# Reordering the start of a feed-forward block: an accumulating transfer behind a norm, an activation table at the beginning, squares and gated units behind later weights

## The chip, the cores and the metric

The kernel runs on one core of a Trainium2 chip. The metric is the device time of one execution in microseconds (us), as the median of several runs; lower is better. The core has five engines that work side by side and wait for each other through semaphores: TensorE (PE in the profile) multiplies matrices, VectorE (DVE) and ScalarE (ACT) work elementwise, GpSimd (POOL) does small things and issues some DMA transfers, and SyncE (SP) issues most transfers. Each engine executes its own instructions in one order.

## The reference

A trunk of two layers is applied with the same weights to a prompt of 512 tokens and a sample group of 256, each token a vector of 1024. Every layer is: half a SwiGLU feed-forward block, a mixer (attention and gating; not touched here), half a SwiGLU block again. At the end stands a norm. So there are four feed-forward blocks in all:

```python
def rmsnorm(x, g):
    return x * lax.rsqrt(jnp.mean(x * x, axis=-1, keepdims=True) + EPS) * g

def swiglu(h, wg, wu, wd):                      # wg, wu: 1024 x 2816, wd: 2816 x 1024
    return (jax.nn.silu(h @ wg) * (h @ wu)) @ wd

x = x + 0.5 * swiglu(rmsnorm(x, f1_n), f1_g, f1_u, f1_d)
x = x + mixer(rmsnorm(x, mix_n), ...)
x = x + 0.5 * swiglu(rmsnorm(x, f2_n), f2_g, f2_u, f2_d)
```

All of it is in float32.

## The kernel before

The 768 tokens stand side by side as columns, in two **halves** of 384 (`HALVES`, L25); the 1024 features are eight tiles of 128 rows. For float32 accuracy each operand is split in a high and a low part and each product is three matmuls: high by high, low by high, high by low (`mm3`, L230). The weight's parts are made in `wsplit` (L147): ScalarE casts the high part (`whi`, L163) and VectorE subtracts it (`wlo`, L164). So PE needs ScalarE and then VectorE for each piece of 128 x 512 weights, and the third matmul of a product is the first to need `wlo`. There are five buffers for each part.

A feed-forward block (`ffn`, L458) goes through the 2816 hidden features in 11 **pairs** of 256 (`pair`, L509). A pair's products with gate and up weights go over tokens in two halves and features in two halves, and a scheme of the Strassen kind makes seven products of the eight. Their activation operands are named in the trace `b11`, `b21`, `t2`, `t3`, `t1`, `b22` and `n4`, and are sums or differences of halves of x with the gain in them; their weights are sums and differences too (`sums`, L711). A **product** here is one of the seven, for gate and for up, 24 matmuls of 128x384: `p1` (`b11`), `p2` (`b21`), `p6` (`t2`), `p7` (`t3`), `p5` (`t1`), `p3` (`b22`) and `p4` (`n4`). The norm's scale of a token is applied after the products, in the gated units: `hidden(i, half, g, u)` (L579) multiplies gate and up by the scale, takes Silu of the gate and multiplies them. It is three VectorE instructions (L585, L587, L588) and one of ScalarE (L586), and it waits until the norm of that half is known (L581).

The block's start: pairs 0, 1 and 2 (`EARLY = 3`) run `p1` and `p2` before everything else, in the sequence of `ORDER` (L42), so that PE has work while the other operands are made (`feed`, `rest`). Then pair 0 runs `t2`, `t3`, `t1`, `b22`, `n4`, then pair 1 the same five, then pair 2.

- *The norm.* ScalarE squares the eight tiles of a half and VectorE adds seven of them up (`norm_add`, L263); PE sums over rows (`norm_tok`, L282), GpSimd takes the power -0.5 (`power`, L311, the instruction of L314), PE spreads the result over partitions (`norm_spread`, L298, the transposes of L198), and ScalarE copies it to `acc` (L455). In the first block the delays `DELAYS` (L34) say after how much PE work, counted at 0.16 us a matmul, the sums and then the spreading are put into PE's order. The first block's second half of squares is made in `squares` (L435).
- *Weight sums by DMA.* `wsum` (L138) loads one weight with SyncE and adds another to it with an accumulating transfer that GpSimd issues (L144). `load_all` (L525) issues all transfers of a pair: ten plain ones (for pair 0, whose first weights are there already, six) and four accumulating ones.
- *The second stage.* `operands` (L475) makes from a pair's gated units the operands of the down projection, in 11 steps. They are taken one at a time: the next pair calls `next(steps)` after certain of its products.
- *What is put behind a product.* `self.after[p, b]` holds functions that are called right after the up weights of pair p's product b have been split; `later` (L595) files pair 0's gated units of the second half this way.

**What sets the order.** The order of PE is that of the program. The instructions of the other engines are ordered by a list scheduler at build time: of those whose inputs and buffers are ready in its model, the one that the program issued first goes first. `issue_after(i)` adds the condition that what stands in the block comes behind instruction i on the same engine; it is an order and not a wait between engines. `high_priority()` puts an instruction ahead of others. The tiles named `e` (30 of them) and `s` (8) are rings whose buffers become free when the last reader is done.

The lines that set the sequence of the start:

```python
        stages = [pair(p) for p in range(NPAIR)]
        for p in ORDER:
            next(stages[p])
        units = [lambda: next(stages[1]), lambda: next(stages[2])]
        if behind:
            self.after[0, "t1"] = [self.squares] + units
        else:
            self.after[0, "t3"] = units
        self.after[0, "n4"] = [lambda: next(stages[1])]
```

`behind` is true in the first feed-forward block alone.

## Time and profile before

| what | value |
|---|---|
| median of 3 runs | 2585.97 us (2585.16 to 2588.82) |
| the profiled execution | 2585.71 us, of them 2583.9 in the profile's span |
| mean granted clock of PE | 0.997 |
| PE busy | 2557.8 us, 99% of the span |
| DVE busy | 2099.9 us, 81% |
| ACT busy | 1370.6 us, 53% |
| POOL busy | 323.3 us, 13% |

The profile is one execution, taken by the hardware profiler. A row of a timeline has the start in us from the beginning of the span, the duration in us, the engine, the line of the kernel, the operation, output <- inputs, how many such instructions are merged in the row, and in brackets how long the engine was idle before it and what ended that. A row of waits has the sum, the count and the longest. Buffer numbers are left out of the names: `whi` and `wlo` are the two parts of a weight, `t20h` is the high part of the first tile of `t2`. Matmuls are pipelined, so the next one starts before the row's duration is over.

### The profile page before, as it was taken

How to read it: one execution, taken by the hardware profiler on the slowest of the kernel's cores; microseconds unless marked ns; L12 is line 12 of the kernel's file. 1: busy time of each engine (PE TensorE's matmuls, PEld its weight loads, DVE VectorE, ACT ScalarE, POOL GpSimd, SP SyncE). 2: the span in 40 equal slices, each digit the busy share in tenths (PEclk: the TensorE clock that was granted, in tenths of full speed). 3: DMA queues.
4: the chain of work that ended last, by engine and by line, in shares of the span. 5: the costliest groups of instructions: out<-in, count | busy, mean ns of one | idle time of the engine just before them, and what ended most of it. 6: DMA issues, size and time to landing. Idle time of an engine off the chain costs nothing.

```text
span 2583.9 us, 42568 instructions
## 1 busy us (share of the span) xinstructions
PE 2557.8 (99%) x15160; PEld 2499.0 (97%) x15160; DVE 2099.9 (81%) x4206; ACT 1370.6 (53%) x2845; POOL 323.3 (13%) x398
## 2 busy tenths in 40 slices
PE   8999999999999999999999999999999999999998
PEld 7999999988899999999999999998999999999998
DVE  8888788879879778788988878886767598878887
ACT  6544454646756545445654445564555475444553
POOL 1111111000111111110111111102212111101100
PEclk9999999999999999999999999999999999999999
DMA  7655556342146545453565455432222256545451
GB/s 205 167 132 126 122 134 159 113 122 68 58 139 158 144 120 130 123 129 88 144 155 135 115 126 127 123 117 77 62 62 65 87 146 168 129 118 124 122 124 51
DMA packets 187156, 310.88 MB, mean 120 GB/s; under 512 B 31680, under 2 KB 46528, under 8 KB 186944
## 3 DMA queue, kind: packets, MB, share of 16 engines
q1 hardware_dynamic: 149792, 240.75, 29.8%
q0 software_dynamic: 36864, 67.13, 16.7%
q8 instruction: 119, 1.95, 0.3%
q14 instruction: 93, 0.76, 0.1%
q10 hardware_dynamic: 288, 0.29, 0.0%
HBM read 298.65 MB, written 15.07 MB: 121 GB/s over the span
## 4 chain that ended last, share of the span: by engine, by line
PE 93%; DVE 3%; ACT 1%; issue 1%; DMA 1%; POOL 0%; ACTq 0%; DVEq 0%; SPq 0%; POOLq 0%
PE ps_mm L187 61%; PE ps_aux L187 31%; PE ps_aux L198 1%; DVE wlo L164 1%; DMA x<-in_x 0%; DVE ol L251 0%; DMA raw<-in_w 0%; DVE s L713 0%; DVE tmp L397 0%; DVE u L576 0%; ACT xh L960 0%; ACT whi L163 0%; POOL sm L314 0%; ACT p L1157 0%; ACT oh L250 0%
## 5 line engine op out<-in xcount | busy, mean ns | idle before, releaser
L163 ACT CAST whi<-s 128x512 fp32r<-128x512 f32 x508 | 310.6, 620 | 404.1 <-PE ps_mm L187 212.7
L164 DVE TENSOR_TENSOR wlo<-s,whi 128x512 fp32r<-128x512 f32 x508 | 344.7, 688 | 180.3 <-ACT whi L163 163.5
L144 POOL DMA_DIRECT2D s<-in_w x256 | 223.6, 914 | 1468.2 <-DVE wlo L164 407.6
L163 ACT CAST whi<-rawp 128x512 fp32r<-128x512 f32 x344 | 211.5, 620 | 265.4 <-PE ps_mm L187 103.1
L164 DVE TENSOR_TENSOR wlo<-rawp,whi 128x512 fp32r<-128x512 f32 x344 | 235.1, 687 | 24.9 <-ACT whi L163 16.6
L187 PE MATMUL ps_mm<-db,whi 128*128 128x384 f32 (+1 forms) x948 | 242.8, 337 | 0.0
L187 PE MATMUL ps_aux<-dt,whi 128*128 128x384 f32 x880 | 225.7, 337 | 0.0
L187 PEld LDWEIGHTS ps_mm<-db,whi 128*128 128x128 f32 x948 | 171.9, 188 | 0.0
L187 PE MATMUL ps_mm<-db,wlo 128*128 128x384 f32 (+1 forms) x474 | 160.0, 337 | 0.6 <-DVE wlo L164 0.6
L187 PEld LDWEIGHTS ps_aux<-dt,whi 128*128 128x128 f32 x880 | 159.8, 188 | 0.0
L187 PE MATMUL ps_aux<-dt,wlo 128*128 128x384 f32 x440 | 148.4, 337 | 0.0
L187 PE MATMUL ps_mm<-xh,whi 128*128 128x512 f32 (+1 forms) x416 | 144.2, 347 | 0.0
L163 ACT CAST whi<-raw 128x512 fp32r<-128x512 f32 x164 | 100.5, 620 | 80.3 <-PE ps_mm L187 55.8
L187 PE MATMUL ps_mm<-xh,wlo 128*128 128x512 f32 (+1 forms) x416 | 140.0, 337 | 0.0
L187 PE MATMUL ps_mm<-xl,whi 128*128 128x512 f32 (+1 forms) x416 | 140.0, 337 | 0.0
L164 DVE TENSOR_TENSOR wlo<-raw,whi 128x512 fp32r<-128x512 f32 x146 | 99.1, 688 | 27.7 <-ACT whi L163 26.5
L576 DVE TENSOR_TENSOR u<-ps_aux,u 128x384 f32<-128x384 f32 x176 | 97.4, 553 | 10.4 <-PE ps_aux L187 8.4
L1157 ACT ACTIVATE p<-p,st 128x256 f32<-128x256 f32 (+3 forms) x144 | 69.0, 481 | 53.4 <-DVE st L1152 53.4
L187 PEld LDWEIGHTS ps_mm<-db,wlo 128*128 128x128 f32 x474 | 88.9, 188 | 1.4 <-DVE wlo L164 1.4
L187 PEld LDWEIGHTS ps_mm<-xh,whi 128*128 128x128 f32 x416 | 78.2, 188 | 10.0 <-issue 1.3
L187 PEld LDWEIGHTS ps_mm<-xh,wlo 128*128 128x128 f32 x416 | 78.1, 188 | 9.4
L187 PEld LDWEIGHTS ps_mm<-xl,whi 128*128 128x128 f32 x416 | 78.3, 188 | 7.5
(508 smaller groups left out, 8059.3 us busy)
## 6 DMA issues: line engine op xcount, KB each, us to landing
rawp<-in_w SPq DMA_DIRECT2D x384, 256.0 KB, 3.2
s<-in_w SPq DMA_DIRECT2D x256, 256.0 KB, 2.9
s<-in_w POOLq DMA_DIRECT2D x256, 256.0 KB, 4.8
raw<-in_w SPq DMA_DIRECT2D x163, 256.0 KB, 2.9
xdm<-x SPq DMA_DIRECT2D x16, 384.0 KB, 2.4
x<-in_x SPq DMA_DIRECT2D x16, 192.0 KB, 4.7
x<-xdm SPq DMA_DIRECT2D x8, 384.0 KB, 3.8
tab<-skew SPq DMA_DIRECT2D x8, 256.0 KB, 4.6
```

The lines of the kernel that those rows point to most:

```text
L144: self.nc.gpsimd.dma_start(f, y, accum_op=ALU.add)
L163: i = nc.scalar.copy(hi, src).ins
L164: self.behind = i, (eng or nc.gpsimd).tensor_tensor(out=lo, in0=src, in1=hi.bitcast(F32), op=ALU.subtract).ins
L187: self.nc.tensor.matmul(out, lhsT=lhsT, rhs=rhs, start=start, stop=stop, **kw)
L198: self.nc.tensor.transpose(out, src, self.ident)
L576: nc.vector.tensor_tensor(out=t, in0=bank[key, n], in1=t, op=ALU.add)
L1157: nc.scalar.activation(outs[i - n0], outs[i - n0], AF.Exp, scale=-1.0, bias=mn[:, i : i + 1], accum_out=sm[:, i : i + 1])
```

## The change

Four places are edited.

1. `wsum`: pair 0's accumulating transfers are ordered behind the norm's last power on GpSimd (`self.powered`).
2. `build`: the first ScalarE activation of the program, on a small tile that nothing reads, is a Silu and not a Copy.
3. First block: the second half's squares and the gated units of pairs 1 and 2 go from behind pair 0's `t1` weights to behind its `n4` weights, its last. There the sequence is pair 1's loads and first weight sums (which stood there alone before), pair 1's gated unit, the squares, pair 2's gated unit. The delays of that half's norm go from (9.0, 3.0) to (5.0, 2.0).
4. All blocks: pair 0's gated units of the second half go from behind pair 1's `t2` weights to behind its `t3` weights, and pair 1 takes the steps of `operands(0)` two at a time after `t1`, `b22` and `n4` (up to 12 calls for 11 steps) where it took one at a time from `t3` on (8 calls, and the last three steps at the pair's end).

```diff
-DELAYS = (11.5, 3.0), (9.0, 3.0)
+DELAYS = (11.5, 3.0), (5.0, 2.0)
...
-        self.nc.gpsimd.dma_start(f, y, accum_op=ALU.add)
+        with self.tc.issue_after(self.powered) if self.late and self.powered else nullcontext():
+            self.nc.gpsimd.dma_start(f, y, accum_op=ALU.add)
...
-            self.nc.gpsimd.tensor_tensor(out=y, in0=v, in1=self.minus[:, : y.shape[1]], op=ALU.pow)
+            self.powered = self.nc.gpsimd.tensor_tensor(out=y, in0=v, in1=self.minus[:, : y.shape[1]], op=ALU.pow).ins
...
+            def ahead():
+                for _ in range(2 if p == 1 else 1):
+                    next(steps, None)
+
             def keep(out, key, n):
...
-                if p != 1 or out != "u2":
+                if p != 1:
                     next(steps, None)
 
             def add(key, n, other):
                 t = e[n, other]
                 nc.vector.tensor_tensor(out=t, in0=bank[key, n], in1=t, op=ALU.add)
-                next(steps, None)
+                ahead()
...
-                    self.after.setdefault((1, "t2"), []).append(f)
+                    self.after.setdefault((1, "t3"), []).append(f)
...
                     product(n, a[n, 2, 2], "n4", "Y", False)
-                    next(steps, None)
+                    ahead()
...
+            def second():
+                load_all()
+                if p < EARLY:
+                    with self.tc.issue_after(self.behind[1]):
+                        for n in names:
+                            sums(n, "s2")
...
+                if behind and p == 1:
+                    second()
+                    yield
                 hidden(0, 0, bank["X", "gate"], bank["X", "up"])
...
         units = [lambda: next(stages[1]), lambda: next(stages[2])]
+        ahead = lambda: next(stages[1])
         if behind:
-            self.after[0, "t1"] = [self.squares] + units
+            self.after[0, "n4"] = [ahead, units[0], self.squares, units[1]]
         else:
             self.after[0, "t3"] = units
-        self.after[0, "n4"] = [lambda: next(stages[1])]
+            self.after[0, "n4"] = [ahead]
...
-            self.np_.tile([P, 6], F32, tag="sm", name="first", bufs=3), self.minus, AF.Copy, scale=1.0
+            self.np_.tile([P, 6], F32, tag="sm", name="first", bufs=3), self.minus, AF.Silu, scale=1.0
```

More of the change, by code (lines that the diff above doesn't have):

```diff
@@ L64, in __init__ @@
         self.fed_last, self.after = {}, {}
-        self.late = self.mark = self.turn = None
+        self.late = self.mark = self.turn = self.powered = None
         self.first = []
@@ L667, in pair @@
             if p:
-                load_all()
-                if p < EARLY:
-                    with self.tc.issue_after(self.behind[1]):
-                        for n in names:
-                            sums(n, "s2")
+                if not (behind and p == 1):
+                    second()
                     if p == 1:
```

## The prediction

> **What bounds the kernel now.** I read the page first, then who TensorE (PE) waits for, then the stretches around the long waits, and last the orders on GpSimd (POOL), ScalarE (ACT) and VectorE (DVE) there.
>
> ```profile
> PE 2557.8 (99%) x15160; PEld 2499.0 (97%) x15160; DVE 2099.9 (81%) x4206; ACT 1370.6 (53%) x2845; POOL 323.3 (13%) x398
> ```
> ```profile
> PE ps_aux L198 <- POOL sm L314: 6.2, 3, 3.3
> PE ps_aux L187 <- DVE wlo L164: 5.5, 1, 5.5
> PE ps_mm L187 <- DVE wlo L164: 3.3, 4, 1.3
> ```
>
> PE is the bound, so only its idle time, 26.1 us (2583.9 - 2557.8), and its slow stretches can be won. Two waits, of 3.3 and 5.5 us, stand in the first 60 us. Here are the windows there (busy us and count of PE, PEld, DVE, ACT, POOL; then clock, DMA share, GB/s):
>
> ```profile
> 23.00:26.50 3.50, 0.20 (x3) 0.02 (x1) 2.67 (x6) 1.12 (x3) 3.43 (x4) 1.00 1.05 268
> 26.50:30.00 3.50, 3.50 (x13) 3.50 (x14) 1.97 (x4) 1.92 (x4) 0.00 (x0) 0.55 1.04 201
> 30.00:51.50 21.50, 21.50 (x122) 21.18 (x121) 19.38 (x39) 19.70 (x42) 3.53 (x4) 0.99 0.69 154
> 51.50:57.40 5.90, 0.36 (x3) 0.05 (x2) 5.90 (x14) 1.88 (x5) 0.00 (x0) 0.72 0.00 0
> 57.40:61.00 3.60, 3.60 (x11) 3.60 (x12) 3.60 (x8) 1.53 (x3) 0.00 (x0) 0.50 0.00 0
> 61.00:69.20 8.20, 7.40 (x46) 7.08 (x46) 7.00 (x14) 3.97 (x9) 2.02 (x2) 1.00 0.66 213
> 69.20:90.30 21.10, 21.10 (x121) 21.10 (x120) 19.91 (x39) 12.00 (x24) 2.62 (x3) 1.00 0.68 154
> ```
>
> At full clock a matmul costs 21.10/121 = 0.174 us, a product of 24 of them 4.19. After each long wait the clock is about half for 3.6 us: 11 matmuls where 20.6 would go, 1.7 us lost. And DVE is nearly full: from 23 to 90.3 its idle time is 0.83 + 1.53 + 2.12 + 0 + 0 + 1.20 + 1.19 = 6.9 us. In this stretch it is a second bound right behind PE.
>
> **The change, part by part.**
>
> *Transfers behind the power.* The norm's power (L314) stands on POOL behind the first pair's four accumulating transfers (L144) and overlaps the issue of the last one, while its input, ScalarE's `sm`, is there from 22.2 on:
>
> ```profile
> 22.07 0.15 ACT L294 ACTIVATE sm<-ps_aux 128x3 f32<-128x3 f32 x1
> 21.59 3.74 POOL L144 DMA_DIRECT2D s<-in_w  x4 [18.15 <-DMA s<-in_w]
> 24.16 2.27 POOL L314 TENSOR_TENSOR sm<-sm,minus 128x3 f32<-128x3 f32 x1
> 26.48 0.59 PE L198 MATMUL ps_aux<-ident,sm 128*128 128x128 f32 x3 [3.30 <-POOL sm L314]
> 63.97 1.09 POOL L314 TENSOR_TENSOR sm<-sm,minus 128x3 f32<-128x3 f32 x1 [19.84 <-ACT sm L294]
> 752.88 1.22 POOL L314 TENSOR_TENSOR sm<-sm,minus 128x3 f32<-128x3 f32 x1 [18.01 <-ACT sm L294]
> 760.91 3.66 POOL L144 DMA_DIRECT2D s<-in_w  x4 [6.81 <-DMA s<-in_w]
> ```
>
> Now it starts at 22.3, when its input is there. Its price has two bounds: 1.09 to 1.22 elsewhere, 2.27 here. I take 1.2, since only the 2.27 overlaps a transfer's issue. PE goes on at 23.5 and not at 26.5; the wait shrinks from 3.3 to 0.5 us, and with it goes the slow clock: 2.8 + 1.7 = 4.5 us on PE's side. The four issues move from 21.6 to about 23.5, and the last ends near 27.3; nothing on POOL is behind them before 32. DVE reads the first two from about 30.6 on (34.64 + 0.47 less the 4.48 of the next part), PE's weights need the other two some 3 us later, so each keeps about 6 us to land. Nothing else moves for it: the plain transfers that they add to go out on SyncE as before, and no engine waits on POOL's queue itself. If they land later than that, DVE waits by so much. In the later blocks the four already follow the power (752.88, then 760.91): nothing changes there.
>
> *Silu's table.* DVE stood still twice: 2.36 us for a ScalarE cast queued behind the norm's late copy, and 2.12 for the first Silu, which had to load its table.
>
> ```profile
> 28.03 0.56 DVE L251 TENSOR_TENSOR t21l<-tmp,t21h 128x384 fp32r<-128x384 f32 x1 [2.36 <-ACT t21h L250]
> 32.79 1.28 ACT L586 ACT_TABLE_LOAD   x1
> 34.64 0.56 DVE L588 SCALAR_TENSOR_TENSOR sg<-sg,v 128x384 f32<-128x384 f32 x1 [2.12 <-ACT sg L586]
> ```
>
> Both go, so DVE comes 4.48 us earlier from here on, about as much as PE. The load that ScalarE makes at the start just becomes Silu's: no cost.
>
> *Squares and gated units moved.* Between the low weights of pair 0's third product and those of its fourth, DVE does 14 operations in 6.55 us, 0.47 each; 13 of them are the squares' seven additions and the gated units of pairs 1 and 2 (six). PE waits for what is behind them:
>
> ```profile
> 38.41 0.34 PE L187 MATMUL ps_mm<-t20h,whi 128*128 128x384 f32 x1
> 48.20 0.55 DVE L277 TENSOR_TENSOR acc<-acc,sq 128x384 f32<-128x384 f32 x1
> 54.75 0.55 DVE L251 TENSOR_TENSOR b222l<-tmp,b222h 128x384 fp32r<-128x384 f32 x1
> 56.62 0.68 DVE L164 TENSOR_TENSOR wlo<-s,whi 128x512 fp32r<-128x512 f32 x1
> 57.35 0.69 PE L187 MATMUL ps_aux<-b220h,wlo 128*128 128x384 f32 x1 [5.54 <-DVE wlo L164]
> 61.90 0.69 DVE L164 TENSOR_TENSOR wlo<-rawp,whi 128x512 fp32r<-128x512 f32 x1
> 69.18 0.34 PE L187 MATMUL ps_mm<-t20h,whi 128*128 128x384 f32 x1
> ```
>
> With 13 x 0.47 = 6.1 us moved away and 4.48 won, the fourth product's low weights are made at 56.62 - 10.6 = 46.0 and ready at 46.7. PE begins pair 0's products at 38.41 - 4.5 = 33.9, the fourth at 33.9 + 3 x 4.19 = 46.5, and wants the low weights with its third matmul, at 46.85. It just fits: this wait (5.54 + 1.7) goes.
>
> *Where the wait goes.* The moved operations now stand behind pair 0's last low weights (61.90 - 10.6 = 51.3, DVE free at 51.9) and ahead of pair 1's first ones. PE reaches pair 1 at 33.9 + 5 x 4.19 = 54.85 and wants these at 55.2. DVE has until then: two sums of pair 1's weights (1.2), the 13 operations, one addition of a bank and the three of pair 0's own gated unit, whose products PE ends meanwhile: 1.2 + 17 x 0.47 = 9.2. That gives 61.1, ready at 61.8: a new wait of 6.6 us, then 1.7 of slow clock. If the last three slip behind it is 5.2. I take 6.6, since at the old place all 14 came ahead of a split that was due after them. The pair's ten plain and four accumulating transfers are still issued at this same product, only now ahead of the gated units, which use other engines: no cost, and what hides them is that their first sums follow only after 51.9, as they follow today (61.90) without a wait. PE ends pair 1's first product at 54.85 + 4.19 + 6.6 + 1.7 = 67.3.
>
> The second half's norm comes only then: the squares were moved, and with the new delays (5.0 and 2.0 us counted at 0.16 us a matmul) its sums stand behind pair 1's first product and its spreading six matmuls later, where it was three. From its first matmul to the copy of its result it took 2.74 us (62.95 to 65.69), so the copy is at 70.0, and DVE goes on with the second half's gated units at 70.5 and not 66.20:
>
> ```profile
> 62.95 0.72 PE L187 MATMUL ps_aux<-ones,acc 128*128 128x1 f32 x6
> 65.11 0.54 PE L198 MATMUL ps_aux<-ident,sm 128*128 128x128 f32 x3 [0.80 <-POOL sm L314]
> 65.69 0.48 ACT L455 COPY acc<-ps_aux 128x384 f32<-128x384 f32 x1 [1.30 <-PE ps_aux L198]
> 66.20 0.56 DVE L585 TENSOR_TENSOR u<-u,acc 128x384 f32<-128x384 f32 x1 [1.08 <-ACT acc L455]
> 89.33 1.29 DVE L164 TENSOR_TENSOR wlo<-s,whi 128x512 fp32r<-128x512 f32 x2
> ```
>
> From there to pair 2's first low weights DVE needs 23.1 us today, 1.2 of it idle; 6.2 us of it (two sums, six weights, one gated unit) will be done before 70.5; the new step count puts two splits (0.94) ahead of them. So 70.5 + 23.1 - 1.2 - 6.2 + 0.9 = 87.1 against 89.33: **2.2 us won in the first block**, though PE alone would give 4.9: the norm costs it 0.6 for the sums, 0.3 for spreading and 0.80 - 3 x 0.174 = 0.3 of wait, so pair 1's second product stands as if begun at 67.3 + 1.2 = 68.5, against 69.18 + 4.19 = 73.4 today. The difference shows as a wait of some 2 us at pair 2's first product. Without the two splits DVE gives 3.1, and with the shorter new wait (5.2) 1.4 more: bounds of 2.2 and 4.5. I take 2.8, near the low end, because the old orders hold to the sequence in which the work is issued.
>
> *Steps and gated units of pair 1, in all four blocks.* Pair 0's second gated units go from behind the first product's weights to behind the second's:
>
> ```profile
> 804.01 0.55 DVE L585 TENSOR_TENSOR u<-u,acc 128x384 f32<-128x384 f32 x1
> 807.46 3.09 DVE L164 TENSOR_TENSOR wlo<-s,whi 128x512 fp32r<-128x512 f32 x5
> 808.20 0.45 PE L187 MATMUL ps_mm<-t30h,wlo 128*128 128x384 f32 x1 [1.34 <-DVE wlo L164]
> 2132.29 0.45 PE L187 MATMUL ps_mm<-t30h,wlo 128*128 128x384 f32 x1 [1.31 <-DVE wlo L164]
> 823.93 1.29 DVE L164 TENSOR_TENSOR wlo<-s,whi 128x512 fp32r<-128x512 f32 x2
> 826.67 0.55 DVE L251 TENSOR_TENSOR db<-u,db 128x384 fp32r<-128x384 f32 x1
> 824.91 0.34 PE L187 MATMUL ps_mm<-t20h,whi 128*128 128x384 f32 x1
> ```
>
> Six operations (2.8 us from 804.01) leave the place ahead of the weights that PE waits for: 1.34 + 1.31 = 2.65 us go. Against it, pair 0's operand splits start a product later and all end within pair 1, so two (826.67 is one) come ahead of pair 2's first low weights. Those are ready at 824.6 and wanted at 824.91 + 0.35: slack 0.65. Two splits, and the first split with its difference, which lose an idle place ahead of the third product, are four operations or 1.9 us; with 0.6 of gaps and 0.65 slack a wait of 0.6 is left. Its bounds are 0 (the splits slip behind, as 826.67 does today) and 1.9 (no gap and no slack counts); I take 0.5, in each of the three later blocks: 2.65 - 1.5 = 1.15 won, between -3.05 and 2.65.
>
> *Sum:* 2.8 + 1.15 = 3.95 from the profiled execution's 2585.7: 2581.8. The median shown lies 0.3 above that execution, so **2582 us**, 0.15% faster, which a measurement of this kernel (0.2%, 5.2 us) hardly tells from no change.
>
> **Rivals.** *The backlog dissolves*: pair 1's weights pass the moved work, no wait takes the old one's place. Then DVE's whole idle time (6.9) and 0.6 of slack are won less the two splits: 6.6, with 2.65 from the later blocks 9.2: 2576.8. For it: weights need only a sum and a cast. Against: at the old place nothing passed.
>
> *Slower*: pair 2's first weights become the common stall. If the six gated operations find no idle DVE in pair 1, 4.7 us (2.8 + 1.9) come ahead of them; less 0.65 that is a wait of 4.0 in each of the three later blocks, 12.0 together, against 2.65 + 2.8 won, so 6.6 lost: 2592.5. It outweighs the gains once those waits pass 1.8 us each. For it: DVE shows only 0.6 us of gaps there. Against it: the run of five weights at 807.46 serves three products, and PE waits for its first alone, so DVE can take the six behind it.
>
> *The power stays long*: if 2.27 us is its price beside a busy DVE, the first wait is 1.6, the copy behind it comes 1.1 later, and DVE loses that: 2583.1. The Trainium skill, SBUF — State Buffer, section "SBUF: two separate sides", speaks for this: VectorE with two SBUF inputs and a GpSimd operation that reads SBUF lock each other out of one shared port pair for a whole instruction. Against it speaks the row at 63.97: 1.09, in a window in which DVE was busy for 7.00 of 8.20 us.
>
> **Numbers.** Forecast 0.52, dissolved 0.26, long power 0.12, slower 0.10. The forecast's own range comes from its bounds: gains of 4.5 + 2.65 and of 2.2 - 3.05 make 2579 to 2587. The range for all, 2575.5 to 2588, adds the dissolved case and leaves out the slower one's far part. Faster by over 0.2%: the dissolved case and a fifth of the forecast, whose best bounds reach 7 us, 0.36; slower 0.09, nearly all of that rival; within, the rest, 0.55.
>
> **What would show it.** Right: the power ahead of the four transfers and PE's first long wait under 0.7 us; one table load less; no wait at pair 0's fourth product; one of 5 to 7 us in pair 1's first, with half the clock behind it; the second half's norm copied near 70 us; none at pair 1's second product in blocks 2 and 4, and short ones at pair 2's first. Wrong: no wait of over 2 us in pair 1 (dissolved), transfers that land after DVE wants them, or waits over 1.8 us at pair 2 in the later blocks.

## The result, and the profile after

The changed kernel takes 2595.73 us (median of 6 runs, 2593.56 to 2596.75) against 2585.77 for the kernel before beside it: ratio 1.0034, 95% interval 1.0023 to 1.0044. The forecast was 2582, 13.7 us less; the changed kernel is 10 us slower than the one before. Its profiled execution took 2595.43 us, 2593.7 of them in the span, at the same mean granted clock (0.997).

The page's first part and the waits of TensorE (sum, count, longest):

```profile
PE 2563.3 (99%) x15160; PEld 2498.7 (96%) x15160; DVE 2099.7 (81%) x4206; ACT 1370.1 (53%) x2844; POOL 324.3 (13%) x398
```
```profile
PE ps_mm L188 <- DVE wlo L165: 10.7, 11, 5.4
...
PE ps_aux L188 <- DVE u L581: 3.9, 4, 1.4
...
PE ps_aux L199 <- POOL sm L315: 3.1, 2, 1.8
```

TensorE's idle time went from 26.1 to 30.4 us (2593.7 - 2563.3), and its busy time from 2557.8 to 2563.3 for the same instructions. The two long waits have become one (5.4), but where four waits of `ps_mm` for low weights stood there are eleven, the 5.4 among them, and four for the addition `u` (L581) are new. The start of block 1, by windows (columns as in the prediction) and rows:

```profile
23.00:26.50 3.50, 3.50 (x22) 3.37 (x21) 3.50 (x8) 2.31 (x5) 3.50 (x5) 1.00 0.84 221
...
62.67:69.38 6.71, 6.71 (x23) 6.71 (x23) 4.25 (x7) 1.00 (x2) 0.00 (x0) 0.55 0.62 173
```
```profile
22.16 0.92 POOL L315 TENSOR_TENSOR sm<-sm,minus 128x3 f32<-128x3 f32 x1 [18.16 <-ACT sm L295]
23.03 3.73 POOL L145 DMA_DIRECT2D s<-in_w  x4
...
69.80 1.75 POOL L145 DMA_DIRECT2D s<-in_w  x2 [9.93 <-DMA s<-in_w]
71.00 1.46 POOL L315 TENSOR_TENSOR sm<-sm,minus 128x3 f32<-128x3 f32 x1
```
```profile
56.64 0.45 PE L188 MATMUL ps_mm<-t20h,whi 128*128 128x384 f32 x1 [0.18 <-ACT ps_mm L598]
62.67 0.69 PE L188 MATMUL ps_mm<-t20h,wlo 128*128 128x384 f32 x1 [5.41 <-DVE wlo L165]
72.51 0.54 PE L199 MATMUL ps_aux<-ident,sm 128*128 128x128 f32 x3 [1.24 <-POOL sm L315]
87.95 0.44 PE L188 MATMUL ps_mm<-n40h,wlo 128*128 128x384 f32 x1 [0.81 <-DVE wlo L165]
91.23 0.44 PE L188 MATMUL ps_mm<-t20h,wlo 128*128 128x384 f32 x1 [0.40 <-DVE wlo L165]
105.24 0.44 PE L188 MATMUL ps_aux<-b220h,whi 128*128 128x384 f32 x1 [1.43 <-DVE u L581]
```
```profile
73.60 0.56 DVE L590 TENSOR_TENSOR u<-u,acc 128x384 f32<-128x384 f32 x1 [2.86 <-ACT acc L456]
```

TensorE works through 23 to 26.5, where it stood before. The new stop at pair 1's first product is there, with 6.7 us at a mean clock of 0.55 behind it. The gated units start at 73.60 and not at 70.5. The last three PE rows are waits that the prediction did not have, at pair 1's `n4` and pair 2's `t2` and `b22`. They come again in every block; here block 3, where the kernel before had no wait in pairs 1 and 2:

```profile
1318.27 0.44 PE L188 MATMUL ps_mm<-n40h,wlo 128*128 128x384 f32 x1 [0.75 <-DVE wlo L165]
1321.53 0.45 PE L188 MATMUL ps_mm<-t20h,wlo 128*128 128x384 f32 x1 [0.38 <-DVE wlo L165]
1334.93 0.45 PE L188 MATMUL ps_aux<-b220h,whi 128*128 128x384 f32 x1 [0.99 <-DVE u L581]
```

**Where the time went.** The measure used from here on is the *offset*: how much later TensorE begins a product than the kernel before begins the same one, read from its first matmul in both traces. Pair 2's `b22` in block 3 begins at 1327.40 before and at 1334.93 after, so +7.53. Before the fourth edit acts, at pair 0's `b22`, the offset is -3.60. It is -1.57 after the norm, +2.37 at the end of pair 2 in block 1; +2.69 to +1.01 at block 2's `t3` (the wait that went), +3.61 at its pair 2's end; +4.29 to +7.64 in block 3; +7.99 to +6.39 and then +9.63 in block 4. In short: from the norm on +3.9 in block 1, +2.6, +3.35 and +3.24 in the later ones, against two gains of 1.6 to 1.7.

**The chain in block 2.** First the kernel before, then the changed one:

```profile
813.95 7.61 SPq L134 DMA_DIRECT2D rawp<-in_w  x3
821.65 0.86 SPq L143 DMA_DIRECT2D s<-in_w  x2
```
```profile
816.18 0.69 DVE L164 TENSOR_TENSOR wlo<-rawp,whi 128x512 fp32r<-128x512 f32 x1
```
```profile
814.64 10.64 SPq L134 DMA_DIRECT2D rawp<-in_w  x2
825.38 0.86 SPq L143 DMA_DIRECT2D s<-in_w  x2
```
```profile
824.21 0.69 DVE L165 TENSOR_TENSOR wlo<-rawp,whi 128x512 fp32r<-128x512 f32 x1
...
838.06 0.69 DVE L726 TENSOR_TENSOR s<-s,rawp 128x512 f32<-128x512 f32 x1 [1.35 <-issue]
...
840.68 0.55 DVE L581 TENSOR_TENSOR u<-ps_aux,u 128x384 f32<-128x384 f32 x1
```

The steps are issued ahead of `n4`'s up weights, so VectorE makes their low part at 824.21 and not at 816.18; TensorE waits 0.83 us for it. Their raw buffer stays taken until then: the second of SyncE's two `rawp` loads goes at 824.95, and the plain transfers behind it, for pair 3's sums, go 3.7 us later. The accumulating transfers follow at 829.02 and 831.55 (825.52 and 826.33 before) and land at 834.87 and 837.98. VectorE stands at these sums until then (it goes on at 834.95 and 838.06, after 0.58 and 1.35 us idle; the profile names no releaser for the second, so the landing is read as its cause). The addition behind them, which TensorE needs for pair 2's `b22`, comes at 840.68:

```profile
831.55 0.86 POOL L145 DMA_DIRECT2D s<-in_w  x1 [1.66 <-DVE s L726]
```
```profile
841.28 0.44 PE L188 MATMUL ps_aux<-b220h,whi 128*128 128x384 f32 x1 [0.59 <-DVE u L581]
```

The prediction looked at none of these three: `n4`'s own weights, the buffer, the order behind the sums.

### The profile page after: what moved, and what is told of

Same layout as the page of the kernel before. It is cut to its first block, busy times and chain, and to the rows that moved or that the text cites. A ratio compares the mean times of both kernels' runs of the same rounds, so it can differ in the third digit from the quotient of the medians.

```text
span 2593.7 us, 42552 instructions
## 1 busy us (share of the span) xinstructions
PE 2563.3 (99%) x15160; PEld 2498.7 (96%) x15160; DVE 2099.7 (81%) x4206; ACT 1370.1 (53%) x2844; POOL 324.3 (13%) x398
## 3 DMA queue, kind: packets, MB, share of 16 engines
q8 instruction: 119, 1.95, 0.3%
## 4 chain that ended last, share of the span: by engine, by line
PE 89%; DVE 5%; DMA 2%; issue 2%; ACT 1%; POOL 0%; SPq 0%; ACTq 0%; DVEq 0%; POOLq 0%
PE ps_mm L188 59%; PE ps_aux L188 29%; DMA s<-in_w 2%; PE ps_aux L199 1%; DVE wlo L165 1%; DVE s L726 0%; DVE u L581 0%; DVE ol L252 0%; DMA raw<-in_w 0%; DVE db L252 0%; DVE dt L252 0%; ACT whi L164 0%; DMA x<-in_x 0%; DVE u L593 0%; ACT xh L973 0%
## 5 line engine op out<-in xcount | busy, mean ns | idle before, releaser
L581 DVE TENSOR_TENSOR u<-ps_aux,u 128x384 f32<-128x384 f32 x176 | 97.4, 553 | 10.0 <-PE ps_aux L188 8.2
L726 DVE TENSOR_TENSOR s<-s,rawp 128x512 f32<-128x512 f32 x120 | 82.0, 689 | 11.4 <-issue 5.8
```

The costliest lines, as they stand in the source:

```text
L581: nc.vector.tensor_tensor(out=t, in0=bank[key, n], in1=t, op=ALU.add)
L726: f = lambda o, x, y: self.nc.vector.tensor_tensor(out=o, in0=x, in1=y, op=ALU.add)
```

## Experiments

The theories named in the expectations: A, the fourth edit's doubled steps cost, by their place ahead of weights; B, the third edit's late norm costs; C, the later accumulating transfers cost; D, VectorE has no idle time left there, so any order only moves the wait; E, place alone. Times are medians in us with the ratio to the kernel before, its 95% interval in brackets (the ratio is not the quotient of the two medians). The offsets (us) are at pair 0's `b22` and at pair 2's end in block 1, over pairs 1 and 2 in block 3 (growth), and in block 4 from pair 1's `t1` to pair 2's end (growth; a gain of 1.6 at `t3` ahead of it is marked *).

| kernel | time | ratio | pair 0 `b22` | block 1 end | block 3 | block 4 |
|---|---|---|---|---|---|---|
| changed | 2595.73 | 1.0034 [1.0023, 1.0044] | -3.60 | +2.37 | +3.35 | +3.24* |
| r1_power_silu | 2583.61 | 0.9989 [0.9980, 0.9999] | -3.55 | -3.64 | 0 | -0.1 |
| r1_no4 | 2585.22 | 0.9995 [0.9986, 1.0004] | -3.59 | -1.13 | 0 | 0 |
| r1_only4 | 2598.09 | 1.0046 [1.0029, 1.0063] | -0.14 | +2.85 | +5.82 | +3.53* |
| r1_onestep | 2587.08 | 1.0004 [0.9994, 1.0013] | -2.91 | +2.07 | +0.73 | +0.67* |
| r2_n4first | 2593.76 | 1.0033 [1.0020, 1.0046] | -3.54 | +1.97 | +1.98 | +2.04* |
| r2_t3first | 2583.02 | 0.9987 [0.9977, 0.9997] | -2.85 | -2.84 | 0 | +1.63* |
| r2_allfirst | 2582.81 | 0.9986 [0.9977, 0.9996] | -2.92 | -3.67 | 0 | +1.63* |
| r2_t2first | 2582.76 | 0.9985 [0.9976, 0.9994] | -4.36 | -4.59 | 0 | 0 |
| r3_w2first | 2594.59 | 1.0032 [1.0021, 1.0044] | -4.16 | +2.62 | +3.64 | +3.55* |
| r3_delay | 2584.59 | 0.9990 [0.9980, 0.9999] | -2.95 | -0.89 | 0 | 0 |
| r3_power (one run) | 2581.53 | | -3.36 | -3.56 | 0 | 0 |
| r3_silu (one run) | 2585.18 | | -0.42 | -0.62 | 0 | -0.1 |
| r4_keepfirst | 2596.83 | 1.0040 [1.0025, 1.0054] | -2.68 | +3.36 | +2.45 | +2.47* |
| r4_units | 2586.24 | 0.9997 [0.9988, 1.0007] | -2.39 | -1.23 | +0.86 | +0.67* |
| r4_sqfirst | 2584.66 | 0.9993 [0.9984, 1.0002] | -3.74 | -1.23 | 0 | 0 |
| r5_eight | 2590.14 | 1.0012 [1.0003, 1.0021] | -3.15 | +1.85 | +1.95 | +1.62* |
| r5_power | 2583.78 | 0.9990 [0.9981, 0.9999] | -3.06 | -2.49 | 0 | 0 |

### The edits taken apart

Edits 1 and 2 alone; all but edit 4; edit 4 alone; and edit 4 with one step at a time:

```diff
 # r1_power_silu, on the kernel before: wsum's issue_after(self.powered), AF.Copy -> AF.Silu
 # r1_no4, on the changed kernel
-                    self.after.setdefault((1, "t3"), []).append(f)
+                    self.after.setdefault((1, "t2"), []).append(f)
 # (and one step at a time from t3 on, as before)
 # r1_only4: edit 4's hunks on the kernel before
 # r1_onestep, on the changed kernel
-                for _ in range(2 if p == 1 else 1):
+                for _ in range(1):
```

> The kernel before with edits 1 and 2 alone (accumulating transfers behind the power, Silu first). Theory A (the loss comes from edit 4, pair 1's doubled steps): the first long wait shrinks from 3.3 to under 0.7 us, VectorE's two stops of 2.36 and 2.12 us go, the wait at pair 0's fourth product stays at 5 to 6.5 us, nothing changes in blocks 2 to 4: 2580 to 2583 us. Theory B (the loss comes from edit 3, the moved squares and the later norm): the same. Theory C (the later accumulating transfers are what costs): VectorE waits for them, no gain or a loss, 2585 to 2590 us.

> The changed kernel with edit 4 undone (pair 0's second gated units behind pair 1's t2 weights, steps singly from t3 on). Theory A: the waits at pair 1's n4 and at pair 2's t2 and b22 go in all blocks, blocks 2 and 4 have their waits of 1.3 us again, block 1 keeps 2 to 5 us of its lead: 2580 to 2584 us. Theory B: block 1 still ends with a loss of 2 us or more: 2587 us or more. Theory C: 2587 us or more.

> The kernel before with edit 4 alone. Theory A: the waits at pair 1's n4 and pair 2's t2 and b22 come in all four blocks, 2 to 3.5 us each, less 1.3 in blocks 2 and 4: 2592 to 2597 us. Theories B and C: no loss, or a gain of up to 2.6: 2583 to 2587 us.

> The changed kernel with the one number 2 set to 1: pair 1 takes one step of pair 0's operands after each product (six in all, five at its end) and all else as changed. Theory A: the n4 up weights come before the steps again, the waits at n4 and at pair 2 go, the waits of 1.3 us in blocks 2 and 4 stay away: 2577 to 2583 us. If not the doubling but the later start of the steps and the later gated units cost: 2590 us or more. Theory B: block 1 ends with a loss: 2586 us or more.

C falls: the first two edits win 2.6 us (2583.61 against 2586.22 beside them), and the offset of -3.6 stays to the end. The third edit gives back 2.5 of it (block 1 ends at -1.13): B holds in part. The fourth alone loses 11.9 (2598.09), and without it (r1_no4) nothing is lost in blocks 3 and 4. With one step at a time most of the loss is gone (1.0034 to 1.0004); what is left of it in block 1 stands ahead of pair 2 (+1.38 at pair 1's `t1`, +2.07 at the end).

### The first block

The first edit alone and the second alone:

```diff
 # r3_power, r5_power: on the kernel before, edit 1 only
+        with self.tc.issue_after(self.powered) if self.late and self.powered else nullcontext():
+            self.nc.gpsimd.dma_start(f, y, accum_op=ALU.add)
 # r3_silu: on the kernel before, edit 2 only
-            ... name="first", bufs=3), self.minus, AF.Copy, scale=1.0
+            ... name="first", bufs=3), self.minus, AF.Silu, scale=1.0
```

> The first edit alone. TensorE's first long wait (3.30 us) should shrink to 0 to 0.6 and pair 0's first product begin some 4.5 us earlier. VectorE still waits for the first Silu's table (2.12 us), but not for the cast behind the norm's copy. If the two edits are each worth half (2.36 and 2.12 us of VectorE's time), pair 0's fourth product waits longer than 5.5 us, about 7 to 8, and the block ends 1 to 2 us earlier than before. If the first edit gives all, it ends 3.5 us earlier, as with both.

> The second edit alone. TensorE's first wait stays at 3.3 us. VectorE gains 1.3 to 2.1 us at the first Silu. The wait at pair 0's fourth product (5.5 us) shrinks by as much, to 3.4 to 4.2, and the first block ends 1.3 to 2.1 us earlier. If ScalarE makes something else late in its place, or VectorE waits for something else (the gated units' inputs), nothing is won.

> The first edit alone, timed (one look gave 2581.5, and the first block ended 3.6 us earlier, as with the first two edits, 2583.6). If the second edit adds nothing, 2582 to 2584, ratio 0.998 to 0.9993 against the kernel before; if ScalarE's table load of 1.28 us still counts, 2584 to 2586.

The first edit has all of the gain: -3.56 in one execution, -2.49 in another, with the second -3.64; their times (2583.78, 2583.61) are not told apart. The second alone wins 0.6, not 1.3 to 2.1. VectorE's rows with edit 1 alone, then with both:

```profile
31.26 0.56 DVE L589 SCALAR_TENSOR_TENSOR sg<-sg,v 128x384 f32<-128x384 f32 x1 [1.40 <-ACT sg L587]
...
35.90 0.55 DVE L252 TENSOR_TENSOR t30l<-tmp,t30h 128x384 fp32r<-128x384 f32 x1
```
```profile
31.46 0.69 DVE L714 TENSOR_TENSOR s<-s,raw 128x512 f32<-128x512 f32 x1 [0.48 <-DMA s<-in_w]
...
34.94 0.69 DVE L165 TENSOR_TENSOR wlo<-s,whi 128x512 fp32r<-128x512 f32 x1 [0.44 <-ACT whi L164]
35.55 0.55 DVE L252 TENSOR_TENSOR t30l<-tmp,t30h 128x384 fp32r<-128x384 f32 x1
```

The 1.40 us at the table's load go, and 0.92 come back as waits for the accumulating transfers, which now land later (ScalarE's cast ahead of the last low part waits 0.59 for one of them too). At `t30l` 0.35 us are left. So the second edit hid a load behind which the data were not there anyway.

Next, pair 1's `t2` weights put ahead of the moved squares and gated units, and two variants:

```diff
 # r2_t2first: r1_no4, with pair 1's t2 weights in high_priority() in block 1
 # r3_delay: r2_t2first, t3's weights too, and
-DELAYS = (11.5, 3.0), (5.0, 2.0)
+DELAYS = (11.5, 3.0), (9.0, 3.0)
 # r4_sqfirst: r2_t2first, and
-            self.after[0, "n4"] = [ahead, units[0], self.squares, units[1]]
+            self.after[0, "n4"] = [ahead, self.squares] + units
```

> The changed kernel without the fourth edit (2585.2 when timed), with the first block's weights for pair 1's t2 put ahead of the moved squares and gated units. The wait of 5.4 us at pair 1's first product should go. If the second half's norm then sets the order (its sums stand behind this product in TensorE's program, and their squares are made last), TensorE waits 4 to 6 us at the sums instead and the block ends within 1 us of the kernel without the edit: 2584 to 2586.5. If what the third edit gave back (2.3 us) came from the weights being late, the time falls to 2581.5 to 2583.5.

> r2_t2first (first three edits, pair 1's t2 weights ahead of the moved work, 2582.8), with pair 1's t3 weights ahead of it too, and the second half's norm sums put 9.0 and 3.0 us of TensorE's work after the squares, as in the kernel before, and not 5.0 and 2.0. There TensorE waited 3.78 us at these sums and 1.59 at the power. If TensorE was only sent to the sums too early, these waits shrink to under 1.5 us together and the first block ends 2 to 4 us earlier: 2579 to 2581. If VectorE is the bound there (its idle time in this stretch is 2.26 us, at the norm's copy), at most 2 us are won, and a wait comes at pair 1's t1 or b22: 2581 to 2584.

> r2_t2first with the squares ahead of pair 1's gated unit and not behind it. Three of VectorE's operations (1.4 us) leave the place ahead of the last square, so the wait of 3.78 us at the norm's sums should be 2.4 or less (1.4 us or more won: 2580 to 2582) if only the order counts. If the gated units behind it free the banks or buffers that something needs, a wait comes at pair 1's t2, t1 or b22 instead: 2582 to 2584.5.

TensorE's waits in these three, in that order:

```profile
62.04 1.44 PE L188 MATMUL ps_aux<-ones,acc 128*128 128x1 f32 x6 [3.78 <-DVE acc L278]
65.07 0.90 PE L199 MATMUL ps_aux<-ident,sm 128*128 128x128 f32 x3 [1.59 <-POOL sm L315]
```
```profile
64.66 1.44 PE L188 MATMUL ps_aux<-ones,acc 128*128 128x1 f32 x6 [4.47 <-DVE acc L278]
67.68 0.90 PE L199 MATMUL ps_aux<-ident,sm 128*128 128x128 f32 x3 [1.59 <-POOL sm L315]
```
```profile
58.80 0.44 PE L188 MATMUL ps_mm<-t20h,whi 128*128 128x384 f32 x1 [2.46 <-ACT ps_mm L598]
...
71.08 0.69 PE L188 MATMUL ps_mm<-t30h,wlo 128*128 128x384 f32 x1 [3.19 <-DVE wlo L165]
```

With its weights ahead, the third edit gives nothing back (-4.36 at pair 0's `b22`, -4.59 at the block's end; edits 1 and 2 alone -3.55 and -3.64), but wins hardly anything either: what it gave back came from the weights being late, and the wait moved to the norm's sums. r3_delay did not test the delays. In all three kernels TensorE's program has the sums right behind `t2`'s gate half, whatever the delays say: the gated units stand behind `t2` there, they need the norm, and so they call for it. Its other change, `t3`'s weights ahead, makes the squares later (4.47) and costs 2.1 us (-2.95 to -0.89). r4_sqfirst likewise trades 3.78 at the sums for 2.46 and 3.19 and loses 2.5 (-3.74 to -1.23). Whatever is put ahead, 5.5 to 7 us of waiting stay between 55 and 72 in these three.

> As r2_t3first, and in the first block also all of pair 0's weights ahead of the squares and the gated units of pairs 1 and 2 (these stay at their old place in the program). If the wait of 5.5 us at pair 0's fourth product comes from the order alone (theory A), it goes; VectorE's work is the same, so a wait of 4 to 6 us comes at pair 1's weights or at the norm's sums, and the first block ends within 1.5 us of r2_t3first: 2579.5 to 2583. If the moved work dissolves in VectorE's idle places, no wait over 2 us is left before 100 us and the time is 2576 to 2579. If moving it costs something by itself, as the third edit did (2.3 us given back), 2583 to 2586.

All of pair 0's weights ahead of the squares in edit 1 and 2's kernel: a wait of 4.50 stays at pair 0's `b22`, now for the operand `b222l` that the weights pushed back. The backlog did not dissolve; the block ends 0.8 us better than in r2_t3first.

### The fourth edit

Ever more of pair 2's work ahead of the doubled steps (each line adds to the one above it):

```diff
 # r2_n4first: on the changed kernel, pair 1's n4 weights ahead
-                    if early and b in ("b11", "b21") or p == 0 and ...:
+                    if early and b in ("b11", "b21") or p == 0 and ... or p == 1 and b == "n4":
 # r3_w2first: and pair 2's t2, t3, t1 weights, and the sums for t2
+                        with self.tc.high_priority() if p == 2 else nullcontext():
 # r4_keepfirst: and pair 2's bank copies
+                with self.tc.high_priority() if p == 2 else nullcontext():
+                    nc.scalar.copy(e[n, out], bank[key, n])
```

> The changed kernel with one addition: the weights of pair 1's last product (n4) are put ahead of other work on the engines (high priority), all else as changed. Theory A (the doubled steps are issued ahead of these weights, VectorE makes them 8 us later, and everything behind them, pair 2's first sums and gated additions, is late) expects that the waits at pair 1's n4 (0.81, 0.83, 0.75, 0.70 us) and at pair 2's b22 (1.43, 0.59, 0.99, 0.92) go below 0.3 and the time falls to 2586 to 2590. Rival D (VectorE is full there: the work was only taken earlier, and whatever is made behind it is late, whichever weight that is) expects waits of the same sum elsewhere in pairs 1 and 2 (0.5 to 2 us a block) and 2593 to 2597.

> The changed kernel with the weights of pair 1's n4 and of pair 2's t2, t3 and t1 all put ahead of other work, and the sums from which pair 2's t2 weights are made too, so that the doubled steps can only be made behind them. Putting n4's alone ahead only moved the wait to pair 2's t2 (1.26 us there in each block, 2593.8). Theory E (the place of the doubled steps ahead of these weights is what costs; the amount of VectorE's work up to the end of pair 2 is that of the kernel before) expects the waits in pairs 1 and 2 below 0.4 us, a growth of the offset of under 1 us in a block, and 2584 to 2588. Rival D (VectorE has no idle time left there, and any order only moves the wait to the next weight) expects a wait of 0.6 to 2 us at pair 2's b22, n4 or pair 3's first product in each block and 2590 to 2595.

> r3_w2first (the changed kernel with pair 1's n4 weights and pair 2's t2, t3 and t1 weights and sums ahead of other work, 2594.6), and pair 2's copies of its banks t2 and t3 on ScalarE put ahead too, since TensorE waited for the first of them (1.75 to 1.82 us in each block) and it stood right behind the cast of the last step. Theory E (the place of the doubled steps on the in-order engines is all) expects no wait over 0.4 us in pairs 1 and 2 from t1 on, a growth of under 1 us in a block and 2584 to 2589. Rival D (the work ahead of pair 2 is too much, wherever it stands) expects the wait at the next thing made behind the steps, pair 2's b22 or pair 3's first products, again 0.6 to 2 us a block, and 2590 to 2595.

The wait in block 4 with each (and, in r4_keepfirst, what ScalarE did in block 3):

```profile
2156.49 0.44 PE L188 MATMUL ps_mm<-t20h,wlo 128*128 128x384 f32 x1 [1.26 <-DVE wlo L165]
```
```profile
2160.62 0.44 PE L188 MATMUL ps_mm<-t30h,whi 128*128 128x384 f32 x1 [1.78 <-ACT u L575]
```
```profile
2161.97 0.44 PE L188 MATMUL ps_mm<-t30h,whi 128*128 128x384 f32 x1 [1.80 <-ACT u L576]
```
```profile
1325.67 0.51 ACT L251 CAST dn<-sg 128x384 fp32r<-128x384 f32 x1 [0.35 <-DVE sg L472]
1326.09 0.47 ACT L576 COPY u<-ps_mm 128x384 f32<-128x384 f32 x1
```

A's numbers fall (2586 to 2590 were expected of r2_n4first). The waits at `n4` and `b22` went, and 1.26 us came at pair 2's `t2`; in blocks 3 and 4 the growth fell to 1.98 and 2.04, so the place of `n4`'s weights is 1.2 to 1.4 of it. With those weights ahead too, 1.8 us came at `t3`, because ScalarE's copy of the bank stands right behind the cast of the last step (`dn`), and that waits for VectorE. r4_keepfirst did not do what it says: the cast and the copy stand in the same order as in r3_w2first. So E in its pure form (no step ahead of anything in pair 2) was not tried. Each of the three kernels shows a wait that moves, as D has it, though in r3_w2first it came at `t3`, which D had not named, and r4_keepfirst is 1.8 us above D's range.

Then the edit in pieces, on kernels that leave pair 2 alone:

```diff
 # r4_units: r2_t2first, gated units behind t3, seven single steps
-                    self.after.setdefault((1, "t2"), []).append(f)
+                    self.after.setdefault((1, "t3"), []).append(f)
-                if p != 1 or out != "u2":
+                if p != 1 or (n, out) == ("up", "u3"):
 # r5_eight: the changed kernel, no steps after n4
-                    ahead()
+                    if p != 1:
+                        ahead()
 # r2_t3first: edits 1 and 2, pair 1's t2 and t3 weights ahead, gated units left at t2
```

> r2_t2first (2582.8) with the fourth edit's first part alone: pair 0's gated units of the second half behind pair 1's t3 weights, the steps one at a time as before (seven before the pair's end, where it was eight). In blocks 2 and 4 the waits of 1.3 us at t3 go (1.6 us each with what follows them). If the doubled steps cause all the loss, nothing comes instead, and blocks 1 and 3 do not change: 2579.5 to 2581. If VectorE has no idle time left before pair 2's weights (rival D; putting pair 1's t3 weights ahead gave back all of it there), waits of 0.3 to 0.9 us come at pair 2's t2 and t3 in all four blocks: 2583 to 2586.

> The changed kernel, but pair 1 takes no steps after n4: eight steps (two after each product of t1 and b22), and the last three, h22's split, the last difference and its split, at the pair's end as in the kernel before. If these three ahead of pair 2's first weights are the loss (what the prediction priced at 0.5 us a block), the waits at pair 2's t2 and b22 shrink below 0.4, the growth of the offset in block 3 falls from 3.3 us to under 1.2 and the time to 2586 to 2590. If the eight earlier steps and the late n4 weights do it (VectorE has no idle time left), block 3 still grows by 2 us or more and the time is 2591 to 2595.

> The first two edits alone (2583.6 when timed), and pair 1's weights for t2 and t3 put ahead of other work instead of moving the gated units behind t3. If what those units cost is only their place ahead of t3's weights (theory A), the waits of 1.3 us at pair 1's t3 in the second and fourth block go and nothing comes instead: 2580.5 to 2582.5, against the kernel before 0.9978 to 0.9986. If VectorE is full there (rival D), a wait of 0.5 to 1.3 us appears at a later product of pairs 1 or 2 in each, and the time stays at 2583 to 2586.

Block 3 in r5_eight, then block 4 in r2_t3first:

```profile
1317.08 0.45 PE L188 MATMUL ps_mm<-t20h,whi 128*128 128x384 f32 x1 [0.33 <-ACT whi L164]
1318.02 0.45 PE L188 MATMUL ps_mm<-t20h,wlo 128*128 128x384 f32 x1 [0.31 <-DVE wlo L165]
1320.66 0.44 PE L188 MATMUL ps_mm<-t20h,wlo 128*128 128x384 f32 x1 [0.25 <-DVE wlo L165]
```
```profile
2145.70 0.44 PE L188 MATMUL ps_mm<-t20h,wlo 128*128 128x384 f32 x1 [0.50 <-DVE wlo L165]
2148.31 0.44 PE L188 MATMUL ps_mm<-t20h,wlo 128*128 128x384 f32 x1 [0.23 <-DVE wlo L165]
```

In blocks 3 and 4 the loss adds up: gated units behind `t3` 0.86 and 0.67; eight steps two at a time 1.95 and 1.62; all eleven 3.35 and 3.24. So the three last steps are 1.4 and 1.6 of it, a bit under half; without them the waits at `n4` and `b22` are gone, and SyncE's transfers in block 2 go at 822.36 (821.65 before, 825.38 changed). Neither expectation was met: the waits at `t2` fell below 0.4 as the first says, but the loss did not fall under 1.2, nor stay at 2 or more. The rest looks like D's: in r2_t3first, with no step moved at all, the 1.6 us won at `t3` in block 4 come back as short waits at pair 2's `t2` (+1.63). Two stops of 0.50 and 0.23 and a start 0.29 late suffice, because each stop costs some 0.28 us beside its wait: the 1.31 at `t3` cost 1.60. The rows show where it comes from: a matmul's row lasts 0.34 at a pitch of 0.174, so 0.17 of overlap is lost at a stop, and the first row behind it lasts 0.44.

D has a limit, though, that VectorE's idle time between the starts of pair 1's `t2` and pair 2's `t2` shows. In blocks 2 and 4 it is 0.65 and 0.60 us before and 0.17 and 0.25 in the changed kernel, as D says. In block 3, which lost most, it is 3.93 before and 4.87 after, in gaps like this one, ahead of pair 1's weights:

```profile
1305.17 0.69 DVE L165 TENSOR_TENSOR wlo<-s,whi 128x512 fp32r<-128x512 f32 x1 [1.40 <-ACT whi L164]
```

Only from 1308 on, where the steps begin, does VectorE run without a gap. No kernel here puts work into the gaps ahead of that, so it is not shown that order alone could win nothing in block 3.

## Why the prediction was wrong

Point by point:

1. **First wait.** Predicted 0.5 and a power of 1.2; it went, the power took 0.92. Right, and the clock stays at 1.00; pair 0's first product begins 4.64 us earlier (4.5 predicted). The long-power rival falls: that power ran with VectorE at work without a gap, on a low part with two inputs among others (row of the changed kernel, without a bracket):

```profile
22.25 0.69 DVE L165 TENSOR_TENSOR wlo<-raw,whi 128x512 fp32r<-128x512 f32 x1
```

   The Trainium skill's rule (SBUF — State Buffer, "SBUF: two separate sides") would have the two lock each other out; no lengthening shows here.
2. **VectorE 4.48 earlier.** Wrong in its second half: the first edit brought 3.38 at `t30l` (39.28 to 35.90), the table 0.35 more, since "each keeps about 6 us to land" left no slack where the table's wait had been.
3. **Pair 0's fourth product.** Its wait went. Right.
4. **New wait of 6.6 (5.2 if three slip).** 5.41, in the right place. Right in its mechanism; none of the three slipped (VectorE makes 16 operations, theirs among them, from 54.44 to 61.91), and it is shorter than 6.6 because TensorE came 1.8 later.
5. **Norm's copy at 70.0, gated units at 70.5.** 73.09 and 73.60. TensorE came to pair 1 at 56.64 and not 54.85, which the wait covers, but it ended 0.9 later than 61.8; the slow clock cost 2.9 us (22 matmuls to 69.38 in 6.71 us, 3.83 at full clock) and not 1.7; and the power stood on POOL behind two accumulating transfers (69.80, then 71.00), so sums to copy took 3.71 and not 2.74. From 73.60 on the step "70.5 + 23.1 - 1.2 - 6.2 + 0.9" gives 90.2, and VectorE began pair 2's first low weights at 90.49: the sum was right, its start was not. **2.8 won became 2.4 lost** at pair 2's end. Without the fourth edit (r1_no4) the block ends with 1.13 won, so 1.7 of these 5.2 are the first three edits' and 3.5 the fourth's, which point 7 is about.
6. **Waits at pair 1's `t3`.** They went, and were worth 1.68 and 1.60, not 1.34 and 1.31. Right.
7. **The step that failed:** "I take 0.5, in each of the three later blocks". Measured 2.6, 3.35 and 3.24; in the first block, where 0.9 was put down for two splits, 3.5. The three steps taken after `n4`, two of which the estimate was about, are 1.4 and 1.6 of it in blocks 3 and 4 (r5_eight). The bounds (0 to 1.9) counted only what comes ahead of pair 2's first low weights. They left out `n4`'s own up weights in pair 1 (0.70 to 0.83 us a block), the raw buffer that these hold, SyncE's queue, and the addition behind the late sums (0.59 to 1.43).
8. **The slower rival** had VectorE's lack of idle time as its mechanism and pair 2's first weights as its place: 12.0 in the three later blocks, 2592.5. Measured 9.2, over several places. The loss of each block is past its point of decision (1.8 us), but the waits at pair 2's `t2` are not (0.25 and 0.38 in block 3): they stayed as short as the forecast had them, so that sign of being right came true while the time did not. With a chance of 0.10 it was held too unlikely, on the reason that "PE waits for its first alone, so DVE can take the six behind it": where these six were moved with single steps (r4_units), pair 2 lost 0.86 and 0.67 in blocks 3 and 4.

The balance against 2581.8: block 1 5.2 us (2.8 won, 2.4 lost), the later blocks 7.1 (+1.15 predicted; 3.3 - 9.2 = -5.9 measured), and 1.4 between the blocks, in stretches without waits. Together 13.7; measured 2595.4 - 2581.8 = 13.6.

The dissolved backlog did not come: one wait of 5.41 stands in pair 1. The least that any order left between 30 and 76 us was 5.0 us, in six waits (r4_units; 6.3 in the kernel before); it had won 0.8 by pair 1's `t1` and lost 2.0 in pair 2.

Not settled: how much of the loss a true order with every step behind pair 2's copies would leave; that needs another way to order ScalarE than priority. Nor is it settled what steps in VectorE's gaps ahead of pair 1's weights would give in block 3.

The best kernels tried take the first edit and leave the steps alone: 2582.76 (r2_t2first), 2582.81, 2583.02, 2583.61 and 2583.78 (the first edit alone), each faster than the kernel before with an interval that ends below 1, and not told apart among themselves.

## What to carry to other kernels

Before moving work to an earlier place in the program, list all that its engine makes behind the new place up to where the old one was, on each engine it touches, and what buffers those results free: here a weight's low part that was made 8 us later, and for which TensorE waited 0.8, held a queue of loads 3.7 us longer. Where the second engine was busy without gaps next to the bound, a wait removed by order alone came back behind it, in whole or in part, in every kernel here that tried it; that suggests less work there as the gain, which no run tried. So look first where that engine does have gaps. An edit that ends an engine's wait for a third party (the power behind transfer issues) is of another kind, and that one held in every kernel here.

## What the runs showed of the hardware

**The half clock after a stop begins and ends at different times.** Edit 1's kernel stopped 5.51 us at the same matmul in both its profiles; the windows behind it (r3_power, then r5_power):

```profile
56.00:60.00 4.00, 4.00 (x24) 4.00 (x23) 4.00 (x9) 0.64 (x2) 0.00 (x0) 0.85 0.20 66
```
```profile
56.00:60.00 4.00, 4.00 (x16) 4.00 (x16) 4.00 (x8) 0.94 (x2) 0.00 (x0) 0.60 0.18 65
```

24 matmuls against 16, and 0.8 us of the offset (-3.36 to -3.56, against -3.06 to -2.49). The granted clock is 0.5 for 6.83 us in both, but from 50.41 to 57.23 in the first and from 52.35 to 59.18 in the second: it falls 2.0 and 3.6 us after the stop has begun, and the work behind the stop runs at it for 3.3 and 4.9 us. In the changed kernel it is 0.5 from 61.94 to 68.77, for 6.1 us of work; in r1_power_silu, behind a stop of 5.51 too, only from 53.43 to 56.85. In all traces here such a stretch, but for the one at the program's end, is 3.41, 6.83 or 10.24 us long. The Trainium skill (TensorE: Matmul & The Clock Gate, "Part 1: The HAM clock gate") has the gate judge activity in windows of some 3.4 us that run on by themselves, so that the time to the next release depends on where in a window the work begins; stretches of one, two and three times 3.41 us, and two phases behind one stop, agree with that. By its rule a stop of a whole window brings the half clock; here one of 1.82 us did, in r3_w2first's block 3 (PE's row at 1324.71), for 3.4 us and 1.65 us of offset:

```profile
1326.70:1328.70 2.00, 2.00 (x8) 2.00 (x7) 1.93 (x5) 0.97 (x3) 0.00 (x0) 0.50 0.83 208
```

Two short stops can also bring it: 0.43 and 1.26 us within 2 us, in r2_n4first's block 2, and nothing after nearly the same two (0.34, 1.26) in its block 3:

```profile
828.00:832.00 4.00, 4.00 (x16) 4.00 (x15) 3.43 (x7) 1.76 (x4) 0.00 (x0) 0.57 0.95 232
...
1321.00:1325.00 4.00, 3.73 (x21) 3.73 (x22) 4.00 (x8) 2.33 (x5) 0.00 (x0) 1.00 0.53 151
```

**The matmuls' pitch differs between executions at a granted clock of 1.00**: in a stretch with TensorE never idle, 573 matmuls in 100 us of the kernel before, 569 in r4_units, whose offset grew by 2.7 us between blocks 2 and 3 without a stop (-2.08 to +0.61). One program does so too: between the same blocks edit 1's kernel kept its offset in one profile (-4.20) and lost 0.7 us in the other (-2.97 to -2.29). Offsets across such a stretch are not the edit's; within pairs 1 and 2 of one block they are, to some 0.2 us (in the changed kernel's block 2 the offset goes from +1.01 to +0.81 without a stop).

```profile
960.00:1060.00 100.00, 100.00 (x573) 100.00 (x572) 79.69 (x143) 47.91 (x94) 10.40 (x12) 1.00 0.50 124
```
```profile
960.00:1060.00 100.00, 100.00 (x569) 100.00 (x568) 79.02 (x142) 47.57 (x94) 10.39 (x12) 1.00 0.49 121
```
